# An encoder block on one core: one bank and one copy for a group's sums of p·v, sums last in a step, three score banks, other places for the mixes, four banks for the last feed-forward tile

## The chip, the core and the metric

The kernel runs on one core of a Trainium2 chip. A core has TensorE (PE in the profile), VectorE (DVE), ScalarE (ACT), GpSimd (POOL) and SyncE (SP), which issues most of the transfers between HBM and the on-chip memory SBUF. TensorE writes its products into PSUM, eight banks of 128 partitions by 512 float32; VectorE and ScalarE read them there. The metric is device time of one execution in microseconds, lower is better.

## The reference

One layer of an encoder for 2048 positions of 1024 channels in float32. The block computes x + W_out[norm(attention), norm(Fourier mix)] of the normed input, then adds a gated feed-forward network, then norms again.

```
w = norm(x) @ w_in                       # q, k, v (768 each), fourier (256)
for window, dilation in ((128, 1), (512, 4), (2048, 16)):        # three branches
    s = q k^T / 8 + bias, masked to |j| <= window / (2 * dilation), keys strided by dilation
    m = max(s);  p = exp(s - m);  l = sum(p);  o = p v / l;  lse = m + log(l)
attn = sum over branches of softmax(lse over branches) * o       # 12 heads of 64
h = x + [norm(attn), norm(fourier_mix)] @ w_out
y = norm(h + (silu(conv3(norm(h) @ w_gate)) * (norm(h) @ w_val)) @ w_down)   # width 2816
```

## The kernel before

Most products are made of float16 pairs: a number is split into a high and a low half, and `mm3` (L239 to L241) issues three matmuls, high by high, high by low and low by high, into one float32 sum.

**Attention.** Twelve heads go in six pairs, numbered 0 to 5. A pair has 40 groups, and `step` is called once for each group: 0 to 15 for the first branch, 16 to 31 for the second, 32 to 39 for the third (the last pair takes the branches in the order second, third, first). A group is one head's two query tiles of 128 against 256 keys, or in the third branch four tiles against 128 keys. A group stays in the pipe for five steps. In its own step TensorE writes its scores into PSUM tiles named `s` (`scores`, L985; the step of the first head writes both heads', so it is the longer one of two), VectorE adds the bias and takes the negative maximum (L990, one instruction and one read of its result for each piece), and ScalarE takes the exponential (`expo`, L998). Two steps later TensorE transposes p into a tile `pt` (`turn`, L1003), ScalarE writes its high half (L1005) and VectorE its low half (`rest`, L1010) to `pT`. One step after that TensorE multiplies with the values into `av` (`sums`, L239 to L241, 65 columns a tile, the last the sum of p), and in the next step the sums are copied to a tile `R` in SBUF (`rows`): ScalarE copies the first two tiles (L1036), and where there are four, VectorE the others (L1034). Scores, `pt`, `av` and the fill products `mm` have two banks each.

TensorE is kept busy by fill units, three matmuls of 512 columns each, 0 to 2 in a step as `share` says: the q and k projections of the next pair, in the last pair the output products of the Fourier branch, whose results VectorE adds (L1419). When eight units have completed a chunk of q or k, ScalarE writes its high and VectorE its low half in the same step (`split`, L191 and L192).

`in_order` (L246) ties every engine to the order in which the program issues. What stands in which step is written out by `plan`: `at(n, f)` calls f ahead of step n's own work. So in pairs 1 to 5 the three branches of the pair before are mixed, a quarter of the positions at a time. `others` loads the rows of the other two branches (`Ro`, by SP from `acc_d`); `mix` calls `weigh` (five VectorE instructions, L1045 to L1049, on 8 numbers a partition); one step later ScalarE takes an exponential, and two steps later `merge` has eight VectorE instructions (L1058 to L1064) and five of 512 numbers a partition on GpSimd (L1067, L1069). The pair's own mixes of the last pair follow in its last steps, and after them rows are copied (`m_copy`, L1471), squared, normed and transposed (`m_turn`, L1502) for the output projection. In step 29 of pairs 0 to 3 `qk_scale` (L172 to L636) scales the next but one projection weights on VectorE; `qk_max` (L609) prepares it in steps 21 and 24. The tile's pool hands a buffer to its next user when the readers of the last one are done.

**Last feed-forward tile.** The feed-forward network goes over 22 tiles of 128 of its 2816 channels. `last_tile` multiplies the last tile's values in four chunks of 512 positions (L1639), takes the product with the gate (L1768) and its maximum (L1769) on VectorE, and finds the maximum over all partitions with a transpose (L1776) ahead of the down projection (`d`). The PSUM tiles of this part are W, X, Y and Z, of 1024 columns, two banks, each. Chunks 0 and 1 go into the halves of W, chunks 2 and 3 into those of Y. Ahead of the value work of chunk 1, VectorE has the preparation of the down projection's scales.

Of the kernel before, what the change touches and what calls it, by code (L numbers as in the profile page):

```python
# [22 lines left out]
HD = 64  # L23
# [129 lines left out]
class Block:  # L153
# [498 lines left out]
    def qk_units(self, p):  # L652
# [4 lines left out]
        def part(c, i, k):  # L657
            sl = slice(c * 512, (c + 1) * 512)
            if k == 0:
                keep["o"], keep["w"] = self.mmtile(), self.wq[i]  # L660
            o, w = keep["o"], keep["w"]
            self.mm3(o, w[:, 0, k], w[:, 1, k], hT[:, 0, k, sl], hT[:, 1, k, sl], k == 0, k == KT - 1)
            if k < KT - 1:
                return
            if c == 0:
                t = qp.tile([128, 2, S], F16, name="qk"[i], bufs=2 - i)
                self.qk[p] = self.qk.get(p, []) + [t]
            t = self.qk[p][i]
            self.split(t[:, 0, sl], t[:, 1, sl], o, 2.0 ** -19)

# [49 lines left out]
    def plan(self, p):  # L720
# [37 lines left out]
        if p:  # L758
            for q4, load, mix in ((0, 4, 7), (1, 5, 10), (2, 11, 14), (3, 14, 17)):
                at(load, lambda q4=q4: self.others(p - 1, q4))  # L760
                at(mix, lambda q4=q4: self.mix(p - 1, q4, self.nc.gpsimd, 3))
        if last:
            for q4, load, mix in zip(QUARTERS, (28, 29, 36, 40), (33, 36, 40, 44)):
                at(load, lambda q4=q4: self.others(p, q4))
                at(mix, lambda q4=q4: self.mix(p, q4, self.nc.gpsimd, 1))
            at(20, self.m_gains)

            for n in range(4):
                at(24 + n, lambda n=n: self.m_load(n))
            for n, g in enumerate((38, 39, 44, 44)):  # L770
                at(g, lambda n=n: self.m_square(n, self.at.tile([128, 512], F32, name="mo", bufs=2)))
            late = lambda n, fn: self.lates.setdefault(40 * p + n, []).append(fn)
            for i, g in ((0, 40), (2, 44)):
                late(g, self.m_rsqrt)
                for n in (i, i + 1):
                    late(g + 1 if n == 1 else g, lambda n=n: self.m_norm(n, self.ss[:, n % 2:n % 2 + 1]))
            for n in range(2):
                at(42 + n, lambda n=n: self.m_turn(n, [self.ps.tile([128, 512], F32, name="pt", bufs=2) for _ in range(2)]))
                at(43 + n, lambda n=n: self.m_load(4 + n))
            for k in range(6):  # L780
                at(14 + 2 * k + 4 * (k // 5), lambda k=k: self.wo_load(k))

    def share(self, p, n):

        if p + 1 == self.pairs:
            return 2 if 3 < n < 24 and (n % 2 or n >= 16) else 1
        if n < 32:
# [3 lines left out]
    def attention(self, hT):  # L791
# [27 lines left out]
        us = list(self.fourier)  # L819
        for i in range(5):  # L820
            for fn in self.timers.pop(self.G, []):
                fn()
            n = -(-len(us) // (5 - i))
            self.step(None, None, us[:n])
# [39 lines left out]
    def step(self, new, fin, units):  # L864
# [15 lines left out]
        if new:  # L880
            new[1]()
        if back(3):
            back(3)[4]()
        for u in units[1:]:
            u()

# [54 lines left out]
    def group(self, p, h, b, tiles, R, t0, two):  # L941
# [33 lines left out]
        def scores():  # L975
            if h == 0:
                for i in range(2):
                    two[i] = ps.tile([128, 512], F32, name="s", bufs=2)
                k = self.qk[p][1].rearrange("p x (r s) -> p x r s", r=1) if b == 0 else self.ks[p, b]
# [33 lines left out]
        def sums():  # L1013
            pT = keep["pT"]
            keep["av"] = []
            for j0 in range(0, len(plan), 2):
                av = ps.tile([128, 512], F32, name="av", bufs=2)
                keep["av"].append(av)
                for j in range(2):
                    o, wd, _, pieces = plan[j0 + j]  # L1020
                    a = j * (HD + 1)
                    for (pp, _, _, blocks) in pieces:
                        for i, n in enumerate(blocks):
                            c = slice(o + i * 128 + pp.start, o + i * 128 + pp.stop)
                            d = av[pp, a:a + HD + 1]
                            self.mm3(d, pT[:, 0, c], pT[:, 1, c], vb[:, n, h, :HD + 1], vb[:, n, h, HD + 1:],
                                     i == 0, i == len(blocks) - 1)

        def rows():
            for i, av in enumerate(keep["av"]):  # L1030
                dst = R[:, t0 + 2 * i:t0 + 2 * i + 2, h, :HD + 1]
                src = av[:, :2 * (HD + 1)].rearrange("p (j v) -> p j v", j=2)
                if i:
                    nc.vector.tensor_copy(dst, src)  # L1034
                else:
                    nc.scalar.activation(dst, src, AF.Copy)  # L1036

# [705 lines left out]
    def last_tile(self, j, gt, val, inv, past, first, prod, bank, ga):  # L1743
# [16 lines left out]
        for c in range(4):  # L1760
            o = bank["WY"[c // 2]][:, c % 2 * 512:(c % 2 + 1) * 512]
            x = slice(c % 2 * 512, (c % 2 + 1) * 512)
# [11 lines left out]
        nc.vector.tensor_tensor(m, m, self.a_top, op=OP.max)  # L1774
        t = ps.tile([128, H], F32, name="X")
        nc.tensor.transpose(t[:1, :128], m, self.eye)  # L1776
# [439 lines left out]
```

## Time and profile before

| | |
|---|---|
| median of 3 runs (lowest to highest) | 2355.49 us (2355.14 to 2358.22) |
| the profiled execution | 2353.07 us |
| its span | 2351.1 us |
| TensorE busy | 2239.8 us, 95% |
| VectorE busy | 1679.9 us, 71% |
| ScalarE busy | 991.6 us, 42% |
| GpSimd busy | 733.5 us, 31% |
| attention, about | 296 to 925 us of the span |

The shares are averages over a projection, the attention and a feed-forward part that differ in what limits them. An engine's idle time has to be read in one stage, with what it waited for.

### The profile page before, as it was taken

Reading aid. Unit: us, or ns where it says so; the run is one execution under the profiler, and the core shown is the slowest. Engines: PE = TensorE matmul, PEld = TensorE weight load, DVE = VectorE, ACT = ScalarE, POOL = GpSimd, SP = SyncE. Lnnn points to the kernel's source line nnn. Section 1 sums busy time; section 2 is a strip of 40 time slices with the busy share of each in tenths; the row PEclk is TensorE's granted clock in tenths of the full one; section 3 lists DMA queues with packets and bytes.
Section 4 is the critical chain, followed back from the end, with each engine's and each line's share of the span. In section 5 each row is a group of like instructions: output and inputs, shape, how many; then the busy total and the mean of one; then the engine's idle time right before and its main releaser. Section 6 shows DMA issues by size and latency. Waiting matters only on the chain.

```text
span 2351.1 us, 39484 instructions
## 1 busy us (share of the span) xinstructions
PE 2239.8 (95%) x15173; PEld 1209.9 (51%) x15173; DVE 1679.9 (71%) x3415; ACT 991.6 (42%) x1841; POOL 733.5 (31%) x697
## 2 busy tenths in 40 slices
PE   6999999999899988999999999999999989999997
PEld 3657866566565654444444444444444434444443
DVE  4656768888978797774777878778777669654454
ACT  5433467576676763543322222222222235432222
POOL 1112122442515233331121212212122226656655
PEclk8999999999999998999999999999999989999999
DMA  3434434252534696971122121221222234343222
GB/s 133 143 101 124 129 96 132 72 140 68 149 102 109 199 294 211 244 200 45 36 90 91 62 90 54 81 90 45 90 67 69 99 111 140 116 142 105 95 90 81
DMA packets 281705, 266.46 MB, mean 113 GB/s; under 512 B 62102, under 2 KB 244014, under 8 KB 280494
## 3 DMA queue, kind: packets, MB, share of 16 engines
q1 hardware_dynamic: 276302, 245.60, 35.2%
q10 hardware_dynamic: 5216, 18.35, 2.2%
q8 instruction: 119, 1.95, 0.4%
q14 instruction: 68, 0.56, 0.1%
HBM read 176.32 MB, written 86.27 MB: 112 GB/s over the span
## 4 chain that ended last, share of the span: by engine, by line
PE 43%; issue 22%; DVE 16%; POOL 10%; ACT 5%; DMA 3%; SPq 2%; POOLq 0%; DVEq 0%; ACTq 0%
POOL A L1828 6%; PE mm L239 5%; PE mm L241 4%; PE mm L240 4%; PE d L239 4%; PE d L241 4%; PE d L240 4%; PE s L985 3%; DVE s_sb L990 3%; PE pt L1003 2%; PE o L240 2%; PE o L239 2%; PE o L241 2%; SPq L244 2%; ACT A L1827 2%
## 5 line engine op out<-in xcount | busy, mean ns | idle before, releaser
L1639 PEld LDWEIGHTS <-A 128*128 128x128 f16 x3744 | 366.7, 98 | 457.6 <-issue 18.1
L998 ACT ACTIVATE s_sb<-s_sb,R 128x256 f32<-128x256 f32 (+1 forms) x576 | 230.0, 454 | 153.0 <-DVE R L990 151.5
L990 DVE CUSTOM_DVE_ANT_0 s_sb<-s,bias,alpha 128x256 f32<-128x256 f32 (+1 forms) x576 | 216.9, 419 | 52.3 <-PE s L985 51.1
L1639 PE MATMUL X<-h2T,A 128*128 128x512 f16 x1080 | 240.4, 379 | 0.8 <-DVE x L1534 0.8
L1639 PE MATMUL W<-h2T,A 128*128 128x512 f16 x1008 | 226.3, 381 | 7.8 <-DVE val L1768 5.6
L1639 PE MATMUL Y<-T,A 128*128 128x512 f16 x984 | 219.2, 379 | 4.5 <-DVE h2T L1658 2.2
L1828 POOL TENSOR_TENSOR A<-wst_v,A 128x2048 f16<-128x2048 f32 (+3 forms) x46 | 155.4, 3391 | 185.8 <-ACT A L1827 137.9
L241 PE MATMUL d<-wd,aT 128*128 128x512 f16 x540 | 204.7, 379 | 4.9 <-DVE aT L192 4.8
L239 PE MATMUL d<-wd,aT 128*128 128x512 f16 x540 | 204.7, 379 | 0.0
L240 PE MATMUL d<-wd,aT 128*128 128x512 f16 x540 | 204.7, 379 | 0.0
L192 DVE SCALAR_TENSOR_TENSOR aT<-wst_v,a_s,aT 128x896 f16<-128x896 f32 x66 | 87.4, 1324 | 144.4 <-ACT aT L191 144.4
L1010 DVE SCALAR_TENSOR_TENSOR pT<-pt,pT 128x512 f16<-128x512 f32 (+1 forms) x240 | 156.5, 652 | 8.7 <-ACT pT L1005 7.7
L241 PE MATMUL mm<-hT,wqk 128*128 128x512 f16 x384 | 147.3, 384 | 5.1 <-POOL wqk L642 5.1
L191 ACT ACTIVATE aT<-wst_v,a_s 128x896 f16<-128x896 f32 x66 | 68.7, 1040 | 194.6 <-PE d L241 109.6
L239 PE MATMUL mm<-hT,wqk 128*128 128x512 f16 x384 | 149.2, 388 | 0.9 <-ACT wqk L641 0.9
L165 POOL PARTITION_ALL_REDUCE wg_a<-am_g x22 | 8.9, 406 | 450.7 <-DVE am_g L1795 438.8
L1005 ACT ACTIVATE pT<-pt 128x512 f16<-128x512 f32 (+1 forms) x240 | 135.4, 564 | 29.6 <-PE pt L1003 28.6
L240 PE MATMUL mm<-hT,wqk 128*128 128x512 f16 x384 | 147.4, 384 | 0.0
L1003 PE MATMUL pt<-eye,s_sb 128*128 128x128 f32 x900 | 143.1, 279 | 0.1
L985 PE MATMUL s<-k,q 64*128 64x256 f16 (+2 forms) x1908 | 114.0, 254 | 25.1 <-DVE R L990 24.5
L1827 ACT ACTIVATE A<-wst_v 128x2048 f16<-128x2048 f32 (+3 forms) x46 | 73.1, 1593 | 153.1 <-DVE wst_v L1803 130.6
L241 PE MATMUL av<-vb,pT 128*128 128x65 f16 (+1 forms) x960 | 116.8, 194 | 15.6 <-DVE pT L1010 15.6
(472 smaller groups left out, 4848.8 us busy)
## 6 DMA issues: line engine op xcount, KB each, us to landing
a_d<-val SPq DMA_DIRECT2D x42, 512.0 KB, 3.4
wst_v<-a_d SPq DMA_DIRECT2D x66, 256.0 KB, 3.2
vb<-v_d SPq DMA_DIRECT2D x12, 1040.0 KB, 7.3
wst_v<-w_gate SPq DMA_DIRECT2D x22, 512.0 KB
wst_v<-w_val SPq DMA_DIRECT2D x44, 256.0 KB, 5.0
dws<-w_down SPq DMA_DIRECT2D x22, 512.0 KB, 5.9
wst_v<-w_down SPq DMA_DIRECT2D x11, 1024.0 KB, 5.1
Ro<-acc_d SPq DMA_DIRECT2D x36, 264.0 KB, 3.2
```

Source lines behind the costliest of these rows:

```text
L239: t.matmul(out, lh, rh, start=first, stop=False)
L240: t.matmul(out, lh, rl, start=False, stop=False)
L241: t.matmul(out, ll, rh, start=False, stop=last)
L985: nc.tensor.matmul(two[i][pp, o:o + wd], q[hs, x, qs], k[hs, y, r, ks], start=n == 0, stop=n == 2)
L990: nc.vector.tensor_tensor_reduce(s_sb[:, o:o + wd], s_ps[:, o:o + wd], bias[:, h, bc:bc + wd], alpha[:, 1:2], 3.0e38, OP.add, OP.min, nm)
L998: nc.scalar.activation(s_sb[:, o:o + wd], s_sb[:, o:o + wd], AF.Exp, scale=-1.0, bias=nm)
L1003: nc.tensor.transpose(pt[:, o:o + 128], keep["p"][:, o:o + 128], self.eye)
L1005: nc.scalar.activation(pT[:, 0, :tot], pt[:, :tot], AF.Copy, scale=2.0 ** 14)
L1010: nc.vector.scalar_tensor_tensor(pT[:, 1, :tot], pt[:, :tot], 2.0 ** 14, pT[:, 0, :tot], op0=OP.mult, op1=OP.subtract)
L1639: nc.tensor.matmul(out[:, c - cols.start:c - cols.start + 512], A[:, a, x, k], B[b][:, y, k, c:c + 512], start=first and k == 0 and (x, y) ...
L1827: self.nc.scalar.activation(hi, src, AF.Copy)
L1828: self.nc.gpsimd.tensor_tensor(lo, src, hi, op=OP.subtract)
```

## The change

Ten edits. (1) A chunk of q or k gets its high half at once, its low half one step later. (2) In pairs 1 to 4 the mixes of the pair before move from steps 7, 10, 14, 17 to 8, 15, 22, 29, their loads with them; the last pair keeps the old steps. (3) The last pair's own mixes move from 33, 36 to 34, 37, and that of step 44 makes its five wide instructions on VectorE; squares, norms, transposes and loads behind them move one or two steps. (4) In the last pair step 16 has one unit in place of two. (5) Six steps after the last group in place of five, over which the remaining units are shared out. (6) The sums stand behind all units of a step. (7) Three score banks. (8) One `av` bank takes all sums of a group, up to 260 columns. (9) One ScalarE copy takes them to `R`, and the VectorE copy is gone. (10) The last feed-forward tile's chunks go to W, Y, X and Z, and the last transpose to W.

```diff
@@ qk_units
-            self.split(t[:, 0, sl], t[:, 1, sl], o, 2.0 ** -19)
+            self.nc.scalar.activation(t[:, 0, sl], o, AF.Copy, scale=2.0 ** -19)
+            self.after(1, lambda: self.nc.vector.scalar_tensor_tensor(t[:, 1, sl], o, 2.0 ** -19, t[:, 0, sl], op0=OP.mult,
+                                                                      op1=OP.subtract))
@@ plan
-            for q4, load, mix in ((0, 4, 7), (1, 5, 10), (2, 11, 14), (3, 14, 17)):
+            for q4, load, mix in ((0, 4, 7), (1, 5, 10), (2, 11, 14), (3, 14, 17)) if last else (
+                    (0, 4, 8), (1, 10, 15), (2, 18, 22), (3, 24, 29)):
...
-            for q4, load, mix in zip(QUARTERS, (28, 29, 36, 40), (33, 36, 40, 44)):
+            for q4, load, mix in zip(QUARTERS, (28, 29, 36, 40), (34, 37, 40, 44)):
...
-                at(mix, lambda q4=q4: self.mix(p, q4, self.nc.gpsimd, 1))
+                at(mix, lambda q4=q4, mix=mix: self.mix(p, q4, self.nc.gpsimd if mix < 44 else self.nc.vector, 1))
...
@@ share
-            return 2 if 3 < n < 24 and (n % 2 or n >= 16) else 1
+            return 2 if 3 < n < 24 and (n % 2 or n >= 18) else 1
@@ attention
-        for i in range(5):
+        for i in range(6):
...
@@ step
         if new:
             new[1]()
+        for u in units[1:]:
+            u()
         if back(3):
             back(3)[4]()
-        for u in units[1:]:
-            u()
@@ group, scores
-                    two[i] = ps.tile([128, 512], F32, name="s", bufs=2)
+                    two[i] = ps.tile([128, 512], F32, name="s", bufs=3)
@@ group, sums
-            for j0 in range(0, len(plan), 2):
-                av = ps.tile([128, 512], F32, name="av", bufs=2)
...
+            av = keep["av"] = ps.tile([128, 512], F32, name="av")
...
@@ group, rows
-                if i:
-                    nc.vector.tensor_copy(dst, src)
-                else:
-                    nc.scalar.activation(dst, src, AF.Copy)
+            n = len(plan)
+            nc.scalar.activation(R[:, t0:t0 + n, h, :HD + 1], keep["av"][:, :n * (HD + 1)].rearrange("p (j v) -> p j v", j=n),
+                                 AF.Copy)
@@ last_tile
-            o = bank["WY"[c // 2]][:, c % 2 * 512:(c % 2 + 1) * 512]
+            o = bank["WYXZ"[c]][:, :512]
...
-        t = ps.tile([128, H], F32, name="X")
+        t = ps.tile([128, H], F32, name="W")
```

TensorE's order in a step with two units, pair 1, before; `mm<-hT,wqk` is a unit's product and `av<-vb,pT` a sum of p·v:

```order
L241 LDWEIGHTS wqk_4666
L241 MATMUL mm<-hT,wqk_4666 128x512
L239 LDWEIGHTS pT
L239 MATMUL av<-vb,pT 128x65
L240 LDWEIGHTS pT
L240 MATMUL av<-vb,pT 128x65
```

The same place now:

```order
L241 LDWEIGHTS wqk_4666
L241 MATMUL mm<-hT,wqk_4666 128x512
L239 LDWEIGHTS wqk_4666
L239 MATMUL mm<-hT,wqk_4666 128x512
L240 LDWEIGHTS wqk_4666
L240 MATMUL mm<-hT,wqk_4666 128x512
L241 LDWEIGHTS wqk_4666
L241 MATMUL mm<-hT,wqk_4666 128x512
L239 LDWEIGHTS pT
L239 MATMUL av<-vb,pT 128x65
```

The second unit has moved ahead of the sums.

VectorE's order in pair 1 behind the merge of the first quarter, before; L990 is a piece of the scores, and the rows from L1045 are the next quarter's weigh:

```order
L1064 TENSOR_TENSOR mg_e<-mg_e,mg_r 128x24
L990 ISA s_sb,R_5324<-s,bias_3936,alpha 128x256
L990 ISA R_5324 128x1
L990 ISA s_sb,R_5324<-s,bias_3936,alpha 128x256
L990 ISA R_5324 128x1
L1010 SCALAR_TENSOR_TENSOR pT<-pt,pT 128x512
L1045 TENSOR_TENSOR mn<-R_3354,Ro_5201 128x8
L1046 TENSOR_TENSOR mn<-mn,Ro_5203 128x8
L1049 TENSOR_TENSOR mg_e<-mn,R_3354 128x8
```

Behind the same merge now (L1059, L994 and L1014 are the lines that were L1064, L990 and L1010):

```order
L1059 TENSOR_TENSOR mg_e<-mg_e,mg_r 128x24
L994 ISA s_sb,R_5297<-s,bias_3936,alpha 128x256
L994 ISA R_5297 128x1
L994 ISA s_sb,R_5297<-s,bias_3936,alpha 128x256
L994 ISA R_5297 128x1
L1014 SCALAR_TENSOR_TENSOR pT<-pt,pT 128x512
L671 SCALAR_TENSOR_TENSOR q<-mm,q 128x512
L994 ISA s_sb,R_5297<-s,bias_3936,alpha 128x256
L994 ISA R_5297 128x1
L994 ISA s_sb,R_5297<-s,bias_3936,alpha 128x256
L994 ISA R_5297 128x1
L1014 SCALAR_TENSOR_TENSOR pT<-pt,pT 128x512
```

The weigh of the second quarter is no longer there; it follows five steps later. The low half of a chunk of q (L671) stands by itself, behind a step's scores.

## Rows read from the trace of the kernel before

**Rows 1.** What TensorE waited for, 296 to 1000 us: total, times, longest.

```profile
PE s L985 <- DVE R L990: 24.5, 23, 4.5
...
PE av L241 <- DVE pT L1010: 15.6, 21, 2.4
```

**Rows 2.** Equal stretches, pairs 0-4: length, busy PE, PEld, DVE, ACT, POOL, clock.

```profile
311.21:346.70 35.49, 35.49 (x397) 23.15 (x396) 24.06 (x77) 24.34 (x61) 0.00 (x0) 1.00 0.17 44
405.89:450.69 44.80, 39.04 (x403) 24.79 (x400) 39.34 (x131) 25.03 (x67) 25.43 (x22) 0.96 0.41 108
509.89:553.50 43.61, 38.60 (x403) 24.38 (x400) 38.40 (x130) 24.91 (x67) 25.39 (x22) 0.96 0.43 112
612.68:656.15 43.47, 37.39 (x402) 23.82 (x399) 39.34 (x131) 24.92 (x67) 25.42 (x22) 1.00 0.42 112
715.34:759.58 44.24, 38.88 (x402) 24.35 (x399) 38.10 (x129) 24.99 (x67) 25.44 (x22) 0.96 0.33 87
```

**Rows 3.** Timeline of VectorE, pair 1, steps 8 to 10: start, duration, idle before.

```profile
407.24 0.25 DVE L1049 TENSOR_TENSOR mg_e<-mn,Ro 128x8 f32<-128x8 f32 x2
...
410.53 0.17 DVE L1058 TENSOR_TENSOR mg_l<-mg_e,R 128x8 f32<-128x8 f32 x1
...
411.71 0.18 DVE L1064 TENSOR_TENSOR mg_e<-mg_e,mg_r 128x24 f32<-128x24 f32 x1
...
413.23 0.82 DVE L1045 TENSOR_TENSOR mn<-R,Ro 128x8 f32<-128x8 f32 x1
...
415.26 1.10 DVE L1049 TENSOR_TENSOR mg_e<-mn,Ro 128x8 f32<-128x8 f32 x2
```

**Rows 4.** Timeline of GpSimd in the same stretch, the merge's last instruction.

```profile
416.41 1.17 POOL L1069 TENSOR_TENSOR mo<-mo,Ro 128x512 f32<-128x512 f32 x1
```

**Rows 5.** Timeline of VectorE, pair 1, step 29, the scaling's first and last instruction.

```profile
468.76 0.16 DVE L172 TENSOR_SCALAR wqk_a<-wqk_a 128x2 f32<-128x2 f32 x1
...
471.45 0.14 DVE L636 TENSOR_SCALAR alpha<-alpha 128x1 int32<-128x1 int32 x1
```

**Rows 6.** Costliest groups by shape, 296 to 930 us: busy, mean ns, idle before.

```profile
L998 ACT ACTIVATE s_sb<-s_sb,R 128x256 f32<-128x256 f32 x324 | 150.6, 504 | 138.6 <-DVE R L990 138.1
...
L239 PE MATMUL av<-vb,pT 128*128 128x65 f16 x840 | 106.9, 195 | 1.8 <-ACT R L1036 1.2 <-DVE R L1034 0.3
...
L1036 ACT ACTIVATE R<-av 128x130 f32<-128x130 f32 x240 | 63.1, 263 | 1.6 <-PE av L241 1.6
...
L191 ACT ACTIVATE vrow<-mm 128x256 f16<-128x256 f32 x1 | 0.4, 384 | 0.4 <-PE mm L241 0.4
```

**Rows 7.** A stretch of pair 2, the eight steps of the third branch.

```profile
480.99:497.71 16.72, 16.59 (x247) 12.06 (x243) 15.23 (x76) 16.49 (x49) 2.45 (x2) 1.00 0.54 162
```

**Rows 8.** Timeline of TensorE, pair 1, step 9: transposes and first sum.

```profile
410.77 0.60 PE L1003 MATMUL pt<-eye,s_sb 128*128 128x128 f32 x4
...
411.85 0.19 PE L239 MATMUL av<-vb,pT 128*128 128x65 f16 x1
```

**Rows 9.** Timeline of TensorE, last pair, two waits for scores.

```profile
852.01 0.91 PE L985 MATMUL s<-k,q 64*128 64x128 f16 x23 [3.31 <-DVE R L990]
...
893.53 0.82 PE L985 MATMUL s<-k,q 64*128 64x256 f16 x6 [4.51 <-DVE R L990]
```

**Rows 10.** Timeline of VectorE, last pair, a weigh that waits for its load.

```profile
892.06 0.17 DVE L1046 TENSOR_TENSOR mn<-mn,Ro 128x8 f32<-128x8 f32 x1 [2.19 <-DMA Ro<-acc_d]
```

**Rows 11.** Timeline of TensorE, output projection, transposes of a later tile.

```profile
947.46 0.74 PE L1502 MATMUL t<-eye,mrow 128*128 128x128 f32 x5 [2.72 <-issue]
```

**Rows 12.** Timeline of TensorE, last feed-forward tile, its second chunk.

```profile
1890.81 7.22 PE L1639 MATMUL W<-h2T,A 128*128 128x512 f16 x24 [5.62 <-DVE val L1768]
```

**Rows 13.** Timeline of VectorE, last feed-forward tile, second and last chunk.

```profile
1901.39 0.74 DVE L1768 SCALAR_TENSOR_TENSOR val<-W,wg_i,act 128x512 f32<-128x512 f32 x1
...
1909.43 0.75 DVE L1768 SCALAR_TENSOR_TENSOR val<-Y,wg_i,act 128x512 f32<-128x512 f32 x1 [4.71 <-PE Y L1639]
```

**Rows 14.** A stretch, the first products of the down projection.

```profile
1915.50:1918.90 3.40, 3.39 (x9) 1.17 (x10) 3.37 (x7) 2.83 (x4) 0.00 (x0) 0.55 0.37 98
```

More of the change, by code (lines that the diff above doesn't have):

```diff
@@ L769, in plan @@
                 at(24 + n, lambda n=n: self.m_load(n))
-            for n, g in enumerate((38, 39, 44, 44)):
+            for n, g in enumerate((40, 40, 45, 45)):
                 at(g, lambda n=n: self.m_square(n, self.at.tile([128, 512], F32, name="mo", bufs=2)))
             late = lambda n, fn: self.lates.setdefault(40 * p + n, []).append(fn)
-            for i, g in ((0, 40), (2, 44)):
+            for i, g in ((0, 41), (2, 45)):
                 late(g, self.m_rsqrt)
@@ L777, in plan @@
             for n in range(2):
-                at(42 + n, lambda n=n: self.m_turn(n, [self.ps.tile([128, 512], F32, name="pt", bufs=2) for _ in range(2)]))
-                at(43 + n, lambda n=n: self.m_load(4 + n))
+                at(43 + n, lambda n=n: self.m_turn(n, [self.ps.tile([128, 512], F32, name="pt", bufs=2) for _ in range(2)]))
+                at(44 + n, lambda n=n: self.m_load(4 + n))
             for k in range(6):
@@ L819, in attention @@
         us = list(self.fourier)
-        for i in range(5):
+        for i in range(6):
             for fn in self.timers.pop(self.G, []):
                 fn()
-            n = -(-len(us) // (5 - i))
+            n = -(-len(us) // (6 - i))
             self.step(None, None, us[:n])
@@ L1014, in sums @@
             pT = keep["pT"]
-            keep["av"] = []
-            for j0 in range(0, len(plan), 2):
-                av = ps.tile([128, 512], F32, name="av", bufs=2)
[L1018 to L1027, printed above, removed]
-        def rows():
-            for i, av in enumerate(keep["av"]):
-                dst = R[:, t0 + 2 * i:t0 + 2 * i + 2, h, :HD + 1]
-                src = av[:, :2 * (HD + 1)].rearrange("p (j v) -> p j v", j=2)
-                if i:
-                    nc.vector.tensor_copy(dst, src)
-                else:
-                    nc.scalar.activation(dst, src, AF.Copy)
+            av = keep["av"] = ps.tile([128, 512], F32, name="av")
+            for j, (o, wd, _, pieces) in enumerate(plan):
+                a = j * (HD + 1)
+                for (pp, _, _, blocks) in pieces:
+                    for i, n in enumerate(blocks):
+                        c = slice(o + i * 128 + pp.start, o + i * 128 + pp.stop)
+                        self.mm3(av[pp, a:a + HD + 1], pT[:, 0, c], pT[:, 1, c], vb[:, n, h, :HD + 1], vb[:, n, h, HD + 1:],
+                                 i == 0, i == len(blocks) - 1)
+        def rows():
+            n = len(plan)
+            nc.scalar.activation(R[:, t0:t0 + n, h, :HD + 1], keep["av"][:, :n * (HD + 1)].rearrange("p (j v) -> p j v", j=n),
+                                 AF.Copy)
         return scores, expo, turn, rest, sums, rows
```

## The prediction

> **What bounds the kernel now.** I read the list of waits of TensorE first. In the attention and the output projection TensorE waits 24.5 us before scores (L985) for VectorE's last read of a score bank (L990), and 15.6 us inside the sums of p·v for VectorE's low part of pT (L1010) [rows 1]. So the stalls belong to VectorE, though TensorE is the busier engine. Then I put the same 14 steps (8 to 21) of five pairs side by side [rows 2]. In pair 0, which mixes nothing, TensorE is busy for all of 35.49 us and VectorE for 24.06, which leaves VectorE 11.43 us idle, 0.82 us a step. In pairs 1 to 4 the four mixes of the pair before fall into these steps (the first weigh just ahead of them), and the stretch takes 44.80, 43.61, 43.47 and 44.24 us: together 34.2 us over four times 35.49.
>
> The timeline of VectorE says what a mix costs there. A weigh is five small instructions. Where GpSimd is idle two of them take 0.25 us (407.24), so the five some 0.65. The next weigh takes from 413.23 to 416.36, 3.1 us, with 0.82 us for its first instruction and 1.10 for its last two, of the same shapes [rows 3]. It falls into the GpSimd merge of the quarter before, five instructions like the last one of 1.17 us, which ends at 417.58 [rows 4]; they began when VectorE's part of the merge had ended, and take some 5.6 us. That part takes 1.3 us, from 410.53 to the end of the row at 411.71 [rows 3]. Four mixes at 2.0 to 4.4 us, within ten steps that have 8.2 us free: that is the bound.
>
> By a rule of the Trainium skill (SBUF — State Buffer, Who interferes with whom) GpSimd and the second operand path of VectorE share a port pair that one of them holds alone; the 1.10 against 0.25 us for two agrees with it. By it a mix that meets a GpSimd merge costs 2.4 us more wherever it stands; the first rival works out what that makes here.
>
> **A. Mixes spread over pairs 1 to 4, three score banks, sums last.** The mixes move from steps 7, 10, 14, 17 to 8, 15, 22, 29. They are then seven steps apart, 17 us or more, while a GpSimd merge takes 5.6: a weigh no longer meets one, and costs 0.65. With the merge 2.0 us in seven steps that have 5.7 free. The third bank lets TensorE write scores while VectorE is a group behind (two pieces, 0.8 us), and the sums, now behind all units of a step, need pT one unit (some 0.65 of the 1.08 us below) later. The low part of q/k, one step later, stays one instruction per chunk. If all 34.2 us of excess were these stalls, all would come back. I keep 6.0 of it: in pairs 1 to 3 the fourth weigh (step 29) stands right behind the scaling of the next weights, which itself holds VectorE from 468.76 to 471.52 [rows 5], 2.75 us, and the third merge (24) beside the reduction for their maximum; 3.4 us of VectorE work at one spot, less the 0.8 us of the bank and the slack of a step, leaves an estimated 1.5, and 0.5 for the other, three times. Gain 28.2. If mixes cost VectorE as much in the new places, only the bank's 0.8 for each of 16 mixes comes back: 12.8. Upper end 34.2. I am near the upper end, as pair 0 shows what the steps cost without collisions.
>
> **B. One bank and one ScalarE copy.** VectorE loses its copies for the 48 groups of four tiles (six pairs, eight steps each); ScalarE's 48 grow from 130 to 260 columns. No row has that shape. Against 263 ns for 130 columns stand 384 ns for 256 [rows 6]: 0.96 ns a column, 0.12 us a copy. It matters in branch 2 alone, where the groups have four tiles, and there ScalarE is the full engine: eight steps take 16.72 us with ScalarE busy 16.49 [rows 7]. Of six pairs the last runs these steps under VectorE, so 40 copies count: loss 4.8, between 0 (TensorE, busy 16.59 there, hides it) and 5.8 (all 48). The other branches had one copy of the same size already.
>
> The one bank adds a wait: a group's sums can't start until the copy of the group before is done. Between two groups' sums the shortest step has the transposes and one unit: 410.77 to 411.85, 1.08 us [rows 8]. The copy may stand behind one exponential of 504 ns and takes 263 itself [rows 6]: 0.77. So 0.31 us are left and I take nothing; the second rival has the other end.
>
> **C. Last pair and what follows it.** Its old mix places stay until step 17, and VectorE is the bound there, so the early steps gain nothing. Two long waits for VectorE are 3.31 us at 852.01 and 4.51 at 893.53 [rows 9]. Ahead of the first, the third bank (0.8) and the scores that can then be issued beside the second unit (0.8) run under it: 1.6 (0 to 3.3). The second starts from a load of another branch's rows, awaited 2.19 us by VectorE at 892.06 [rows 10]; one step later in the order, TensorE has a one-unit step more to do meanwhile, estimated 2.0 (0 to 4.5). The extra tail step has no own work: it carries a sixth of the remaining units. After attention the last merge keeps GpSimd for five instructions, 5.6 us by rows 4, before it can copy rows for the output projection, and TensorE waits 2.72 at 947.46 [rows 11]. On VectorE a merge instruction of 512 elements costs some 0.75 (the width of 1901.39, rows 13), 3.7 for five, and GpSimd is free for the copies: I take the 2.7 back (0 to 2.7). Together 6.3, between 0 and 10.5.
>
> **D. Last feed-forward tile.** TensorE waits 5.62 us before its second chunk at 1890.81 [rows 12], because chunk 1 shares a tile with chunk 0, which VectorE reads only at 1890. With a bank each it has no such wait: the four chunks end near 1901, 1890.81 − 5.62 plus three chunks of 5.3. VectorE then sets the end: it comes to chunk 1 at 1901.39 as before, behind the preparation of the down projection, and does three chunks of multiply and maximum at 1.45 us, to 1905.7, where before the last began at 1909.43 [rows 13] and ended at 1910.9. Gain 5.2. TensorE then idles longer before the down projection, whose first products run at a granted clock of 0.55 between the two levels, 2.4 and 1.2 GHz, after such a pause [rows 14]; I take off 0.7 for it (0 to 1.5). 4.5, between 3.7 and 5.2.
>
> **Sum.** 28.2 − 4.8 + 6.3 + 4.5 = 34.2 us. The profiled execution took 2353.07 (span 2351.1), which gives 2318.9; the median, 2355.49, stands 2.4 higher, and with that **2321.3**.
>
> **Rivals.**
> 1. *The stalls only move.* GpSimd's all-reduce for the next weights stands near the third mix, GpSimd merges late, and the weigh at 29 meets it with 2.4 us more behind 2.75 of scaling; qk reductions at 21 and 24 load the same steps. For it: rows 3 and 5. Against: pair 4 prepares no further weights, and seven steps leave VectorE 5.7 us. Half of A goes: +14, 2335.
> 2. *Slower: the single bank becomes the bound.* Of the 240 steps 105 have one unit or none. If the copy ends x us after the 1.08 us of rows 8, each of them loses x: break-even at 34.2/105 = 0.33 us, so a copy 0.64 us later than I worked out. Two more exponentials in front of it (504 ns each, rows 6) would make it 0.7 us late at times; at 0.6 in each of the 105 steps 63 us are lost: 2384. For it: ScalarE is full in branch 2 (rows 7). Against: before, with two banks, a sum hardly waited for a copy (1.8 us in all in the L239 row of rows 6).
> The Trainium skill (PSUM — Partial Sum Buffer, PSUM bank collisions raise a hardware error) wants PSUM guarded by bank, so the next sums can't begin in a part of the bank already copied; no run here shows a finer guard, and this rival is what that costs.
> 3. *Hardly any change.* The spread mixes win 12.8 (lower end of A), B costs 5.8, the wait for the bank costs 0.1 in 105 steps, C gives nothing and D 3.7: 0.2 us gained, 2355. For it: the last pair's places hardly move.
>
> **How the numbers follow.** The forecast case 0.68, rival 1 0.18, rival 2 0.07, rival 3 0.07. A at its upper end and B at nothing make 45.0 us, 2310; C at its upper end besides, 2306. On the other side the range reaches through rival 1, 2335, to where C and D also give only their lower ends, 6.3 and 0.8 us less: 2342, and with B at 5.8, 2343. So 2306 to 2344. A measurement of this kernel tells 0.2%, 4.7 us, from no change. Faster by more than that: forecast, rival 1 and a little of rival 3, 0.87; within it 0.06; slower 0.07.
>
> **What would show it.** In the profile of the changed kernel: the 14-step stretches of pairs 1 to 4 at 35.5 to 38 us (A); a weigh without single instructions near 1 us; the wait of scores for VectorE below 8 us in all; the ScalarE copy of 260 columns near 0.39 us and branch-2 stretches near 17.7 (B); no wait of sums for that copy above some 5 us in all, else rival 2; no wait at 947 for the rows (C); the four chunks of the last tile without a pause, and 4 to 5 us less from there to the down projection (D). The forecast is wrong if the stall of rows 1 turns up under another name in the same stretches, or if steps with one unit grow.

## The result: 1.1% faster, by less than forecast

The changed kernel takes 2332.66 us (median of 4 runs, 2325.34 to 2340.42) against 2356.85: a ratio of 0.9893, interval 0.9874 to 0.9912, so 25 us (21 to 30) are won where 34.2 were forecast. The profiled execution took 2329.35 us with a span of 2327.5; that span is 23.6 shorter than before's.

The same five stretches of 14 steps (8 to 21 of pairs 0 to 4), in the columns of [rows 2]:

```profile
310.53:346.46 35.93, 35.93 (x402) 22.96 (x399) 23.67 (x75) 25.51 (x60) 0.00 (x0) 1.00 0.17 43
406.10:442.02 35.92, 35.92 (x403) 22.97 (x399) 27.36 (x104) 26.13 (x64) 12.85 (x11) 1.00 0.40 106
506.01:541.93 35.92, 35.92 (x403) 22.97 (x399) 27.43 (x104) 26.14 (x64) 12.84 (x11) 1.00 0.44 116
603.78:639.72 35.94, 35.94 (x403) 22.98 (x399) 27.43 (x104) 26.14 (x64) 12.85 (x11) 1.00 0.38 101
703.34:739.27 35.93, 35.93 (x403) 22.98 (x399) 26.82 (x106) 26.12 (x64) 12.84 (x11) 1.00 0.27 72
```

Pairs 1 to 4 now take what pair 0 takes, 32.4 us less than in [rows 2], and TensorE never stops. Pair 0, which mixes nothing, went from 35.49 to 35.93: that loss has another cause. What TensorE waits for in the attention, in the columns of [rows 1], now has one large name in place of two:

```profile
PE av L239 <- ACT R L1030: 27.6, 25, 6.7
```

That is ScalarE's copy of the sums out of the single bank. Pairs 0 to 4 hold 14.2 us of it and the last pair 13.4. Where it comes from in the pairs can be followed at step 30 of pair 1. TensorE first, then ScalarE, then VectorE, then GpSimd:

```profile
467.59 0.19 PE L239 MATMUL av<-vb,pT 128*128 128x65 f16 x1 [1.91 <-ACT R L1030]
```
```profile
466.35 0.91 ACT L1002 ACTIVATE s_sb<-s_sb,R 128x256 f32<-128x256 f32 x2 [4.56 <-DVE R L994]
467.17 0.21 ACT L903 ACTIVATE mg_e<-mg_e 128x24 f32<-128x24 f32 x1
467.28 0.26 ACT L1030 ACTIVATE R<-av 128x130 f32<-128x130 f32 x1
```
```profile
460.39 0.47 DVE L172 TENSOR_SCALAR wqk_a<-wqk_a 128x2 f32<-128x2 f32 x1
460.90 0.97 DVE L174 TENSOR_SCALAR wqk_p<-wqk_a 128x2 int32<-128x2 int32 x1
461.90 0.17 DVE L176 TENSOR_SCALAR wqk_s<-wqk_p 128x2 int32<-128x2 int32 x1
461.97 1.15 DVE L178 TENSOR_SCALAR wqk_i<-wqk_p 128x2 f32<-128x2 f32 x1
...
465.17 0.16 DVE L1040 TENSOR_TENSOR mn<-R,Ro 128x8 f32<-128x8 f32 x1
```
```profile
448.82 0.37 POOL L165 PARTITION_ALL_REDUCE wqk_a<-am_qk  x1 [12.29 <-DVE mg_l L1053]
457.52 1.04 POOL L1062 TENSOR_TENSOR mo<-R,mg_e 128x512 f32<-128x512 f32 x1 [8.33 <-DVE R L994]
...
461.91 1.18 POOL L1064 TENSOR_TENSOR mo<-mo,Ro 128x512 f32<-128x512 f32 x1
```

Read from below: GpSimd runs the all-reduce of step 24, stands for 8.33 us, and only then makes its part of the third merge. VectorE's scaling (0.16 us for its first instruction in [rows 5]) meets it and has instructions of 0.47, 0.97 and 1.15, and the fourth weigh (L1040) stands right behind. ScalarE's exponential waits 4.56 us for the scores, the copy stands behind the exponential, and the next sums wait 1.91 us for the copy.

The longer copy itself is cheap, against [rows 6]:

```profile
L1030 ACT ACTIVATE R<-av 128x130 f32<-128x130 f32 x192 | 51.9, 270 | 15.6 <-PE av L241 14.4
...
L1030 ACT ACTIVATE R<-av 128x260 f32<-128x260 f32 x48 | 18.0, 376 | 1.4 <-PE av L241 1.3
```

By stage, won (+) and lost (−) between the two profiled executions. The bounds are the starts of the transposes of each step, the last product of the output projection, the first value chunk of the last tile and the first product of the down projection:

| stage | us |
|---|---|
| pairs 1 to 4, the 14-step stretches | +32.4 |
| pair 0's stretch and five stretches of 8 steps behind them: 0.03 us a step | −2.0 |
| step 7 (bias scaling), five pairs | −3.8 |
| steps 30 to 34 of pairs 1 to 3 | −7.0 |
| third branch, behind step 34, five pairs | −1.3 |
| last pair | +1.3 |
| after attention to the end of the output projection | +3.8 |
| feed-forward up to the last tile's values | −6.9 |
| last tile to the down projection | +6.4 |
| all else: start of the attention, steps 30 to 34 of pairs 0 and 4, the down projection | +0.7 |

They add up to 23.6. The loss in the feed-forward part lies where nothing was changed. Over 14 profiles (the two here and the twelve below) this part takes 815.5 to 823.6 us, and before happens to hold the shortest. Half of the 6.9 is one wait, 2.16 us before and 5.57 now, and the products behind it run 1.5 us longer (granted clock 0.77 there, between the two levels, and 1.00 before). Before first:

```profile
1853.95 5.34 PE L1639 MATMUL W<-h2T,A 128*128 128x512 f16 x24 [2.16 <-DVE gt L1733]
```
```profile
1834.85 6.86 PE L1634 MATMUL W<-h2T,A 128*128 128x512 f16 x24 [5.57 <-DVE gt L1728]
```

This wait is 2.2 to 3.2 us in the four profiles with the old layout of the last tile and 2.2 to 5.7 in the ten with the new one. For the whole part the three profiles with the old output projection (before, E1, E9) average 817.1 and the other eleven 820.3. So some 3.7 of the 6.9 are spread between executions; whether the other 3.2 are a price of the change stays open.

### The profile page after: what moved, and what is told of

Its sections match the earlier page's. It is cut to its first block, busy times and chain, and to the rows that moved or that the text cites. A ratio compares the mean times of both kernels' runs of the same rounds, so it can differ in the third digit from the quotient of the medians.

```text
span 2327.5 us, 39297 instructions
## 1 busy us (share of the span) xinstructions
PE 2227.7 (96%) x15173; PEld 1199.0 (52%) x15173; DVE 1654.1 (71%) x3372; ACT 1007.4 (43%) x1841; POOL 730.7 (31%) x692
## 3 DMA queue, kind: packets, MB, share of 16 engines
q1 hardware_dynamic: 276302, 245.60, 35.5%
## 4 chain that ended last, share of the span: by engine, by line
issue 21%; PE 15%; POOL 9%; DVE 7%; ACT 4%; DMA 0%; POOLq 0%; ACTq 0%; SPq 0%; DVEq 0%
POOL A L1823 6%; PE d L241 4%; PE d L239 4%; PE d L240 4%; ACT A L1822 2%; PE X L1634 1%; DVE wst_v L1798 1%; DVE wd L192 1%; PE Z L1634 1%; ACT wd L191 1%; POOL sums L1908 1%; POOL sums L1907 1%; POOL sums L1906 1%; POOL sums L1905 1%; DVE wst_v L1802 0%
## 5 line engine op out<-in xcount | busy, mean ns | idle before, releaser
L994 DVE CUSTOM_DVE_ANT_0 s_sb<-s,bias,alpha 128x256 f32<-128x256 f32 (+1 forms) x576 | 217.2, 420 | 77.6 <-PE s L989 76.9
L1634 PE MATMUL W<-h2T,A 128*128 128x512 f16 x984 | 220.6, 381 | 5.6 <-DVE gt L1728 5.6
L1634 PE MATMUL Y<-T,A 128*128 128x512 f16 x960 | 213.7, 379 | 4.5 <-DVE h2T L1653 2.2
L1014 DVE SCALAR_TENSOR_TENSOR pT<-pt,pT 128x512 f16<-128x512 f32 (+1 forms) x240 | 156.8, 653 | 15.9 <-ACT pT L1009 15.4
L1007 PE MATMUL pt<-eye,s_sb 128*128 128x128 f32 x900 | 148.0, 285 | 0.1
L239 PE MATMUL av<-vb,pT 128*128 128x65 f16 (+1 forms) x960 | 116.3, 197 | 28.1 <-ACT R L1030 27.6
L1840 DVE SCALAR_TENSOR_TENSOR act<-gt,cw,act 128x2047 f32<-128x2047 f32 x22 | 81.9, 3723 | 60.4 <-ACT act L1837 60.4
```

The costliest lines, as they stand in the source:

```text
L239: t.matmul(out, lh, rh, start=first, stop=False)
L994: nc.vector.tensor_tensor_reduce(s_sb[:, o:o + wd], s_ps[:, o:o + wd], bias[:, h, bc:bc + wd], alpha[:, 1:2], 3.0e38, OP.add, OP.min, nm)
L1007: nc.tensor.transpose(pt[:, o:o + 128], keep["p"][:, o:o + 128], self.eye)
L1014: nc.vector.scalar_tensor_tensor(pT[:, 1, :tot], pt[:, :tot], 2.0 ** 14, pT[:, 0, :tot], op0=OP.mult, op1=OP.subtract)
L1634: nc.tensor.matmul(out[:, c - cols.start:c - cols.start + 512], A[:, a, x, k], B[b][:, y, k, c:c + 512], start=first and k == 0 and (x, y) ...
```

## The experiments

The times are medians; a ratio is to the kernel before on the same chip. Chips differ by a few microseconds, so runs are compared by their ratios. Stretches are those of [rows 2]; "index" in the expectations counts steps by their transposes, so index 5 is step 7. "The attention" here goes from the first transposes to the end of the last ones, in the profile.

**Places alone, and banks alone.** E1 is the kernel before with the new mix steps, E2 the changed kernel with the old ones (the same lines the other way).

```diff
-            for q4, load, mix in ((0, 4, 7), (1, 5, 10), (2, 11, 14), (3, 14, 17)):
+            for q4, load, mix in ((0, 4, 7), (1, 5, 10), (2, 11, 14), (3, 14, 17)) if last else (
+                    (0, 4, 8), (1, 10, 15), (2, 18, 22), (3, 24, 29)):
```

> The kernel before with the new mix steps alone (8, 15, 22, 29; banks, copies, order and all else as before). Theory 1, that the stalls came from mixes that met each other and GpSimd on VectorE: the 14-step stretches of pairs 1 to 4 fall from 43.5-44.8 to 36-38 us, steps 30 to 34 of pairs 1 to 3 grow by 2 to 5 us each, and the time falls by 18 to 28 us against before. Theory 2, that the third score bank and the late sums give the slack: the stretches stay above 41 us and the gain is below 10 us.

> The changed kernel with the old mix steps (7, 10, 14, 17) in pairs 1 to 4. Theory 1: the stretches go back to 41-44 us, and the time is 18 to 28 us longer than the changed kernel's, near before. Theory 2: the third bank and late sums take the stalls up, stretches stay below 39 us, at most 10 us longer than the changed kernel.

E1: 2358.29, ratio 0.9987 (0.9974 to 1.0). E2: 2346.68, 0.9936 (0.9918 to 0.9954). Neither theory holds. Stretches of E1 with the five steps 30 to 34 behind each, pairs 1 and 2:

```profile
411.78:448.82 37.04, 36.93 (x401) 23.80 (x399) 27.45 (x104) 24.83 (x63) 12.84 (x11) 0.97 0.35 90
469.92:488.00 18.08, 15.38 (x167) 9.62 (x165) 13.66 (x62) 9.84 (x28) 6.02 (x6) 0.81 0.26 74
516.26:553.70 37.44, 37.34 (x403) 23.90 (x400) 27.67 (x106) 25.06 (x64) 12.87 (x11) 0.95 0.37 97
574.80:592.41 17.61, 14.09 (x166) 8.93 (x165) 13.74 (x63) 9.72 (x28) 6.01 (x6) 0.90 0.27 77
```

The stretches fell as theory 1 said, by 29.8 us over four pairs. But steps 30 to 34 of pairs 1 to 3 rose from 12.4 to 17.4-18.1, step 7 from 2.1 to 4.0-4.3, and the attention is as long as before (615.2 against 615.0). The stall had moved whole. In E1, too, GpSimd's third merge starts late:

```profile
456.07 0.37 POOL L165 PARTITION_ALL_REDUCE wqk_a<-am_qk  x1 [12.68 <-DVE mg_l L1059]
463.53 1.03 POOL L1068 TENSOR_TENSOR mo<-R,mg_e 128x512 f32<-128x512 f32 x1 [7.08 <-issue]
```

E2's stretches are 40.3 to 41.2 us, 13.4 less than before in all: the slack of banks and late sums, together with the other edits that it keeps, near the 12.8 that the forecast gave as its lower end.

**Sums early.** E3 is the changed kernel with edit 6 undone.

```diff
+        if back(3):
+            back(3)[4]()
         for u in units[1:]:
             u()
-        if back(3):
-            back(3)[4]()
```

> The changed kernel with the sums ahead of the second unit again. A step with two units took 0.03 us longer in the changed kernel than before (3.00 and 2.13 against 2.97 and 2.10) although TensorE waited for nothing. If the order of sums and units makes this, both go back and about 3.5 us are won over the five pairs, less what sums lose again by waiting for pT's low part (up to 4 us): between 3.5 us faster and 1 us slower than the changed kernel. If it is not the order (another line, the banks), the steps stay at 3.00 and 2.13.

2330.06, 0.9878 (0.9862 to 0.9895). The stretches are 35.5 us in all five pairs and the steps 2.97 and 2.10, so the order makes the 0.03 us a step. Steps 30 to 34 take 14.6 to 16.1, against 13.9 to 16.3: the late sums cover little there. They cover more elsewhere: with sums early steps 22 to 29 of pairs 1 to 3 grew from 20.8 to 21.4, and in this profile the last pair is 4.2 us longer, which was not followed up.

**What steps 30 to 34 wait for.** E4 moves the mixes to 8, 13, 18, 25.

```diff
-                    (0, 4, 8), (1, 10, 15), (2, 18, 22), (3, 24, 29)):
+                    (0, 4, 8), (1, 10, 13), (2, 14, 18), (3, 19, 25)):
```

> The changed kernel with mixes at 8, 13, 18, 25 (loads at 4, 10, 14, 19): the fourth weigh four steps ahead of the scaling, its merge on VectorE two ahead, but GpSimd's part of that merge still behind the all-reduce of step 24. If the stalls of steps 30 to 34 in pairs 1 to 3 (16.3, 14.2 and 13.9 us against 11.95 in pair 0) come from the weigh standing right behind the scaling, they fall to 12 to 12.5 and 7 us are won. If they come from a late GpSimd merge that meets the scaling itself, at most 3 us are won and single small instructions of the scaling still take 0.5 to 1.2 us.

2333.58, 0.9885 (0.9862 to 0.9908): the changed kernel's time. Steps 30 to 34 fell to 13.1, 13.6 and 13.1 us, 4.6 of the 7.0 won, between the two expectations, and 3.2 of that in pair 1. GpSimd's merge is still late, and it still stretches the scaling:

```profile
470.53 0.97 DVE L174 TENSOR_SCALAR wqk_p<-wqk_a 128x2 int32<-128x2 int32 x1
...
471.61 1.16 DVE L178 TENSOR_SCALAR wqk_i<-wqk_p 128x2 f32<-128x2 f32 x1
```

So the weigh, with its merge, behind the scaling is most of the loss; how the rest divides was not taken apart. In pair 1 another collision came up at step 7 (4.75 us). It is the one that the changed kernel has in pair 4. VectorE's bias scaling first, GpSimd's key copies below, and each time the kernel before ahead of the changed one:

```profile
712.00 1.56 DVE L703 TENSOR_SCALAR bias<-bias,alpha 128x512 f32<-128x512 f32 x1
```
```profile
696.97 3.84 DVE L706 TENSOR_SCALAR bias<-bias,alpha 128x512 f32<-128x512 f32 x1
```
```profile
704.93 8.34 POOL L683 COPY k<-k 128x1024 f16<-128x1024 f16 x6
```
```profile
690.20 10.33 POOL L686 COPY k<-k 128x1024 f16<-128x1024 f16 x7
```

The bias scaling takes 0.48 us where GpSimd stands (425.77 in E5, below). Before it met the last of six key copies; here it ends with the last of seven, 3.84 us after its start.

E5 takes all three meetings apart; the last pair of lines, cut from a longer line, is the second branch's bias, with the steps of its load and its scaling.

```diff
-                    (0, 4, 8), (1, 10, 15), (2, 18, 22), (3, 24, 29)):
+                    (0, 4, 8), (1, 10, 13), (2, 14, 18), (3, 19, 23)):
...
-            at(24, lambda: self.qk_max(1))
-            at(29, lambda: self.qk_scale(n + 1))
+            at(26, lambda: self.qk_max(1))
+            at(30, lambda: self.qk_scale(n + 1))
...
-            (1, 34, 46)
+            (1, 34, 54)
```

> The changed kernel with three things moved apart on VectorE: mixes at 8, 13, 18, 23 (loads at 4, 10, 14, 19), the second weight maximum at 26 and the scaling at 30, and the scaling of the second branch's bias in step 14 of the next pair in place of 6. Theory 1b, that what remains are VectorE instructions that meet GpSimd's (the bias scaling the key copies, the weight scaling a late merge): the step stretches at the third bias (index 5) fall from 2.5 and 4.5 us to 2.1, and steps 30 to 34 of pairs 1 to 3 from 16.3, 14.2 and 13.9 us to 12, so attention is some 10 us shorter than in the changed kernel. Rival, that the sum of VectorE's work in these stretches is the bound: the same time turns up elsewhere in the pairs, and attention gains less than 4 us.

2322.47, 0.9842 (0.9818 to 0.9867). The attention is 10.3 us shorter than in the changed kernel (585.1 against 595.4), as theory 1b said: step 7 at 1.49, steps 30 to 34 at 13.4, 12.8 and 12.4. The bias scaling stands clear of GpSimd, whose next instruction starts at 429.54:

```profile
425.77 0.48 DVE L706 TENSOR_SCALAR bias<-bias,alpha 128x512 f32<-128x512 f32 x1
```

E9 gives the kernel before these places and nothing else.

> The kernel before with the places of the last run with things moved apart (mixes 8, 13, 18, 23, weight maximum 26, scaling 30, bias scaling in step 14 of the next pair) and nothing else of the change. Theory 1b, that all stalls of pairs 1 to 4 are VectorE's bunched and colliding instructions, so that no extra bank or late sum is needed once they stand apart: stretches of 14 steps at 35.5 to 36 us, the step of index 5 at 1.5, steps 30 to 34 at 12 to 13, and 25 to 35 us shorter than before. Theory 2b, that places and slack are both needed (the new places alone won 1.5 us): steps 30 to 34 stay above 15 us and the gain is below 12 us.

2330.86, 0.9869 (0.9854 to 0.9885): 31 us won without any bank, copy or order of the change. Pair 1's stretch and its steps 30 to 34, then the scaling's small instructions:

```profile
406.13:442.65 36.52, 35.78 (x402) 23.23 (x399) 29.63 (x113) 23.93 (x63) 16.27 (x15) 1.00 0.50 129
463.61:476.20 12.59, 12.20 (x166) 8.34 (x165) 10.82 (x49) 8.63 (x24) 0.98 (x2) 1.00 0.16 44
```
```profile
464.31 0.17 DVE L174 TENSOR_SCALAR wqk_p<-wqk_a 128x2 int32<-128x2 int32 x1
464.52 0.17 DVE L176 TENSOR_SCALAR wqk_s<-wqk_p 128x2 int32<-128x2 int32 x1
464.60 0.16 DVE L178 TENSOR_SCALAR wqk_i<-wqk_p 128x2 f32<-128x2 f32 x1
```

Once nothing meets, the slack has little to cover: the stretches of pairs 1 to 4 are 36.5 (theory 1b had 35.5 to 36), with 0.74 us of waits in pair 1's, and pairs 0 to 4 take 477.4 us in all where E5 takes 477.1. Theory 2b falls.

**Which bank.** E6 has two score banks and two for the sums.

```diff
-                    two[i] = ps.tile([128, 512], F32, name="s", bufs=3)
+                    two[i] = ps.tile([128, 512], F32, name="s", bufs=2)
...
-            av = keep["av"] = ps.tile([128, 512], F32, name="av")
+            av = keep["av"] = ps.tile([128, 512], F32, name="av", bufs=2)
```

> The changed kernel with two score banks and two banks for the sums (each with all sums of a group, one copy), so only the distribution of banks differs. Theory, that the third score bank is the slack and the single sums bank costs little: waits of scores for VectorE come back, steps 30 to 34 of pairs 1 to 3 go to 16-18 us as in the run with the new places alone, and the time is 5 to 10 us longer than the changed kernel's. Rival, that the single sums bank is what TensorE waits for (27.6 us in all for the ScalarE copy): these waits vanish and little comes in their place, 5 to 10 us shorter.

2333.96, 0.99 (0.9872 to 0.9928), the changed kernel's time; neither expectation. The copy waits vanish and waits of scores (11.8 us) and of pT (16.5) come in their place. The bias scaling met GpSimd again in this profile: it takes 4.79 and 4.80 us in pairs 3 and 4. But the third branch takes 15.94 us where the changed kernel's same steps take 16.97 (pair 0, E6 first):

```profile
383.49:399.43 15.94, 15.94 (x247) 11.78 (x243) 14.23 (x71) 15.94 (x47) 2.14 (x1) 1.00 0.53 149
```
```profile
376.53:393.50 16.97, 16.47 (x248) 11.77 (x243) 14.07 (x69) 16.97 (x50) 2.76 (x2) 1.00 0.58 160
```

So the single copy wins 0.8 us a pair over [rows 7] where it has a second bank. The single bank takes 1.0 back, if the third score bank, which E6 also lacks, costs nothing in these steps; that was not tried by itself.

**ScalarE's order.** E7 issues a group's exponential one step later, behind the next copy.

```diff
-        if new:
-            new[1]()
+        if back(1):
+            back(1)[1]()
```

> The changed kernel with a group's exponential issued one step later, behind the next step's copy and high half on ScalarE. TensorE's waits for the copy (27.6 us) could come from ScalarE's order: the copy stands behind an exponential that waits for VectorE. Theory, that the order ties the copy to VectorE: these waits fall below 12 us and attention is 5 to 12 us shorter. Rival, that VectorE's delay reaches TensorE by another way (the scores' banks, pT's low part) or that the transposes then wait for a late exponential: the waits change their name and attention is within 3 us or longer.

2341.79, 0.9933 (0.9918 to 0.9947), 9 us longer: the rival.

```profile
PE av L241 <- DVE pT L1014: 9.4, 16, 1.0
PE pt L1007 <- ACT s_sb L1002: 6.9, 13, 0.7
...
PE av L239 <- ACT R L1030: 2.0, 1, 2.0
```

The copy's wait fell from 27.6 to 2.0 us, so it was ScalarE's order that carried VectorE's delay there. But the transposes' weight loads wait 2.2 to 2.5 us a pair for exponentials in the third branch, whose eight steps went from 17.0 to 19.8 us in pair 0.

**Tile and merge.** E8 undoes edit 10 and the merge of edit 3 (cut to the main lines).

```diff
-            o = bank["WYXZ"[c]][:, :512]
+            o = bank["WY"[c // 2]][:, c % 2 * 512:(c % 2 + 1) * 512]
...
-                at(mix, lambda q4=q4, mix=mix: self.mix(p, q4, self.nc.gpsimd if mix < 44 else self.nc.vector, 1))
+                at(mix, lambda q4=q4, mix=mix: self.mix(p, q4, self.nc.gpsimd, 1))
```

> The changed kernel with two parts undone that lie in stages of their own: the last feed-forward tile's chunks in W and Y again, and the last merge on GpSimd again. From the first value chunk to the first product of the down projection before took 35.67 us, the changed kernel 29.31. If the shared tiles made the difference, it goes back to 35 to 36; if the other order of work ahead of it did, it stays near 29. From the last transposes of the attention to the last product of the output projection the changed kernel took 146.7 us and before 150.8; if the merge on VectorE made that, it goes up by 2 to 3.5 us, if not, it stays.

2340.31, 0.9933 (0.9914 to 0.9951). The tile takes 35.51 us against 29.31: its layout makes 6.2. From the end of the last transposes to the end of the output projection it takes 152.4 against 146.7, 5.7 longer and more than expected. Of this, 3.75 is one wait, the one of [rows 11]; the changed kernel has none there:

```profile
927.53 0.84 PE L1497 MATMUL t<-eye,mrow 128*128 128x128 f32 x6 [3.75 <-issue]
```

So the merge on VectorE does shorten this part. Its size is less sure: the part takes 150.8 to 153.7 us in the four profiles with the merge on GpSimd, and 146.2 to 150.0 in the ten with it on VectorE.

**Further versions.** E10 is E5 with sums early, E11 E5 with the banks of E6, E12 E11 with sums early and with four loads of the last pair moved behind those that its first own mix waits for.

```diff
-                at(24 + n, lambda n=n: self.m_load(n))
+                at(31 + n, lambda n=n: self.m_load(n))
```

> The changed kernel with the same things moved apart, and the sums ahead of the second unit again. If nothing waits for pT's low part any more, the order's 0.03 us a step comes back: the five stretches at 35.5, some 3.5 us shorter than with the sums late. If the late sums still cover something, waits for pT's low part come up in steps 30 to 34 and it is the same or longer.

> The changed kernel with the same things moved apart, two score banks and two banks for the sums. In the run with these banks alone the eight steps of the third branch took 1.0 us less a pair. If the third score bank covers nothing once the work is apart, that is left: 4 to 5 us shorter than with three score banks and one for sums. If it still covers bursts, waits of scores for VectorE come back and it is the same or longer.

> The changed kernel with the things moved apart, two score banks and two for sums, the sums ahead of the second unit again, and in the last pair the four loads of finished rows (mrow) moved from steps 24 to 27 to 31 to 34, behind the loads of the other branches' rows that the first own mix waits for. Two stages, two questions. Pairs 0 to 4: with sums early the stretches of 14 steps go from 35.9 to 35.5 and those of 8 steps from 20.8 to 20.5, 3.5 us in all, unless waits of sums for pT's low part return. Last pair: TensorE stood 6.0 to 6.7 us at its step 35 while VectorE waited for those rows, with the DMA engines 93 to 98% busy ahead of it; if the order of the transfers makes this, the stall falls below 3 us and nothing comes in its place; if the sum of the transfers does, the stall stays or stands some steps later at the squares. Together 3 to 8 us shorter than the run with two and two banks (2316 us), or within 2 us of it.

E10: 2319.3, 0.9825 (0.9808 to 0.9841). The stretches are 35.5 to 35.6, but steps 30 to 34 are 0.7 us longer than in E5 in pairs 2 and 3; the attention is 2.2 shorter. E11: 2316.03, 0.9805 (0.9787 to 0.9824), attention 5.4 shorter than E5's, a little more than expected. E12: 2311.05, 0.9804 (0.979 to 0.9818). It is the lowest median, but on another chip, and by the ratio E12 and E11 are the same; both are faster than the two kernels. In the profiles E12's attention is 4.9 shorter than E11's, 3.3 of it in pairs 0 to 4. The stall of the last pair stayed: 5.12 us there against 5.96 in E11. So the place of these four loads is not its cause. The sum of the transfers may be, which was not tried: in the changed kernel the DMA engines are 93 to 98% busy from 840 to 870 us, ahead of this wait for the load.

```profile
871.49 0.17 DVE L1040 TENSOR_TENSOR mn<-R,Ro 128x8 f32<-128x8 f32 x1 [4.50 <-DMA Ro<-acc_d]
```

## Why the prediction was right, and where its sizes were off

The direction and the range held (2332.7 in 2306 to 2344), and the first rival, "the stalls only move", with its 2335, came nearest. That nearness is in part luck: the rival takes 14 us from A, where A lost 8.3; 6.9 us in the feed-forward part, of which no term speaks, came on top, and B and D gave some 5 back. The forecast case was right in its first step and wrong in several sizes.

- **A, 28.2 us forecast, 19.9 measured.** That spread mixes clear the stretches was right: 32.4 of 34.2 us, and the 1.8 that are missing are the 0.44 us a stretch that pair 0 lost as well. The sentence "I keep 6.0 of it" was too small, and less by the term that it names than by two that stood at nothing. Steps 30 to 34 of pairs 1 to 3 lost 7.0, 1.0 more than kept; in pairs 0 and 4 they won 0.4. Step 7 lost 3.8. The sums behind all units lost another 3.8: the 1.8 above, and 2.0 outside of these four stretches; E3 shows that it is their order. The 6.0 was near in size, but not in its working: the prediction priced the fourth weigh as an addition to the scaling's 2.75 us, while GpSimd's delayed merge stretched the scaling itself (L172 to the end of L636: 2.83 us before; 4.86, 3.97 and 3.75 in pairs 1 to 3). The rival had named the all-reduce as the reason, but let it hit the weigh. That the weigh behind the scaling matters most is borne out by E4. Step 7 was not seen because moving the first mix from 7 to 8 lets one more key copy of GpSimd run ahead of the merge, beside the bias scaling.
- The bias scaling (L706) takes 3.84 us beside GpSimd's copies and 0.48 apart from them. A rule of the Trainium skill (SBUF — State Buffer, Who interferes with whom) has scaling and copying instructions of VectorE among those that can take the shared pair; the two figures agree with it. The prediction had applied the rule to the weigh alone, though the kernel before already has 1.56 us there.
- **The places need room, and the forecast took the banks' part as a lower end only.** E1, E2 and E9 show what the sum could not: places as they were chosen win next to nothing without slack, slack alone wins 13 us in the stretches, and better places need little slack.
- **B, −4.8 forecast, −1.3 measured.** The copy's price was right (376 ns against the 0.39 us estimated), its effect was not: the third branch's eight steps take 16.97 us in pair 0, where 17.7 were expected. One copy in place of two on two engines wins 0.8 us a pair by E6, and with the banks as they are 1.0 is lost again. That ScalarE was busy for 16.49 of 16.72 us did not mean that a longer instruction on it lengthens the stage.
- **The single bank.** Rival 2's sign came up, 27.6 us of waits for the copy where the prediction allowed 5, but not its loss. In pair 0, where VectorE has no mixes, TensorE waits for it once, 0.37 us in the third branch. Most of the waits are VectorE's delays under another name: with ScalarE's order changed they vanish (E7), and with VectorE's work apart those of pairs 0 to 4 fall from 14.2 to 4.3 us (E5). The last pair keeps its own, 15.4 in E5.
- **C, 6.3 forecast, 5.1 measured.** The parts were wrong, and that they nearly make up for each other is luck: the last pair won 1.3 in place of 3.6, where its first own mix waits for two loads (4.50 and 1.93 us), and the part after the attention 3.8 in place of 2.7.
- **D, 4.5 forecast, 6.4 measured** and 6.2 undone by E8. VectorE does reach chunk 1 behind the preparation, and the three chunks follow in 1.4 us each:

```profile
1883.82 0.74 DVE L1763 SCALAR_TENSOR_TENSOR val<-Y,wg_i,act 128x512 f32<-128x512 f32 x1
...
1886.58 0.74 DVE L1763 SCALAR_TENSOR_TENSOR val<-Z,wg_i,act 128x512 f32<-128x512 f32 x1
```

In before they began at 1901.39 and 1909.43 [rows 13], 8.0 us apart; now 2.8. The clock took little of it back: from the first value product to the first product of the down projection it is 6.4 us shorter, and the rest of the kernel takes 0.3 longer, where 0.7 had been taken off. The down projection's first 3.4 us run at a granted clock of 0.50, which is the lower level, 1.2 GHz, 8.4 us after the end of the last tile's products; before it was 0.55, 6.1 us after them.

A to D measured 30.1 us together. From there to 23.6 it is 6.9 lost in the feed-forward part, 0.7 won ahead of the attention and 0.3 lost from the down projection on. Of the 6.9 the runs show that about half varies from execution to execution.

## What to carry to other kernels

When a stall goes from a stretch, look at the next steps on the same engine before counting it as won: here 30 of 30 us came back in E1 until the work stood clear of everything else on VectorE and GpSimd. Find the slot for a movable instruction by what GpSimd will run at that moment, including the time that it stands behind an all-reduce, and not by the steps of the engine that waits. Extra buffers and better places can buy the same microseconds (E2 and E9); try the places first, since they take no memory.

## What the runs showed of the hardware

- GpSimd stood 6.7 to 8.3 us between the record of an all-reduce and the next ordinary instruction, in all 18 places where its numbers were ready within 0.8 us of that record (6.68 in E6, 7.08 in E1, 8.33 in the changed kernel). The page of the profile calls spans of custom instructions on GpSimd rough, so part of it may be the all-reduce itself; why it stands was not tried.
- A VectorE instruction of 128x512 with a single tensor input grew from 0.48 to 3.84 us beside GpSimd's copies of keys, and one of 128x2 from 0.17 to 0.97 beside its merge.
- The same matmuls take 0.03 us a step more when the sums of 65 columns stand behind the second unit and so right ahead of the transposes (3.00 and 2.13 us against 2.97 and 2.10 in E3), with no wait in the records. Which of the two neighbours makes it was not tried.
